# An expert's ten weight splits in gate and up: from groups to even distances

## The chip, the cores and the metric

The kernel runs on one core of one Trainium2 chip. The metric is the device time of one execution in microseconds; lower is better. The median of three runs of the kernel before is 5451.15 us.

## The reference, cut to what matters

A float32 trunk of two layers on 4096 tokens of 1024 channels. Layer 0 mixes with retention and windowed attention, layer 1 with a Fourier transform; behind each mixer stands a mixture of 32 experts, of which each token takes two, and a layer norm. The change touches the experts alone:

```python
def hierarchical_moe(x, w_coarse, b_coarse, w_fine, b_fine, w_gate, w_up, w_down):
    ...
    xs = xt[tok]                       # the tokens, ordered by expert
    hid = jax.nn.silu(lax.ragged_dot(xs, w_gate, sizes)) * lax.ragged_dot(xs, w_up, sizes)
    ys = lax.ragged_dot(hid, w_down, sizes) * gate.reshape(-1)[order][:, None]
    out = jax.ops.segment_sum(ys, tok, num_segments=T)
...
        x = layer_norm(DEEPNORM_ALPHA * x + ffn, ln2_gain[layer], ln2_bias[layer])
```

## The kernel before

Products are made in float32 by three matmuls on split operands: a value `a` is held as a rounded part `h` and a rest `l = a - h`, and `w*x` is taken as `wh*xh + wh*xl + wl*xh`. `Trunk.split` (L77 to L79) makes such a pair with one Copy on ACT (L78) and one subtraction on DVE (L79).

The class `Experts` (L1437) runs the 32 experts of a layer one after the other, each on a fixed number of token slots (168 to 432). An expert has 12 chunks of weights of 512 KB: w0 to w7 for gate and up, w8 to w11 for down. SP's queue loads them in order into four buffers `raw` (`load`, L1486). `split` (L1492) splits the next chunk into its pair in `w[g % 12]` and, as this frees a `raw`, issues the load of the chunk four places on.

Gate and up (`gate_up`, L1540) are four passes over j; pass j uses w(2j) and w(2j+1) and has eight steps k of six matmuls. So there are 32 steps h = 8j + k. At the end of a pass ACT takes Silu (`hid`, L1556), DVE multiplies by the up part (L1557), and `hid` is split into `hth` and `htl`. Down (`down`, L1564) multiplies these by w8 to w11. Between its products stand the transposes of the next expert's tokens (`trans`, L1518): PE transposes into one of two buffers `pt` (L133), ACT and DVE split that into `xth` and `xtl`.

Before the first expert eight chunks are split. Expert e's own part therefore has twelve splits as follows: its own w8 to w11, then w0 to w5 of the next expert, all ten in gate and up, and w6 and w7 in down. The table `at` in `expert` (L1613) says behind which step each of the ten stands.

The order on each engine is that of the code (`manual_schedule`, `run` L1725): an engine does not pass over an instruction that waits. A split that waits for its chunk on ACT therefore holds up the Silu and the `hth` behind it.

In layer 1 the finishing of tokens (`Done`, `plan` L1244) is put into the experts' steps as well. Experts 1 to 7 carry counts and ranks. From expert 9 on an expert carries one tile of 128 finished tokens, some carry two: statistics on DVE behind step 8 (second tile 12), the scaling on ACT behind 16 (20), the gain on POOL behind 18 (22), the bias on DVE behind 22 (26), the store on POOL behind 24 (28).

Of the kernel before, what the change touches and what calls it, by code (L numbers as in the profile page):

```python
# [1436 lines left out]
class Experts:  # L1437
# [63 lines left out]
    def rows(s, e, t):  # L1501
        return max(0, min(P, s.slots[e] - t * P))
# [110 lines left out]
    def expert(s, e):  # L1613

        ix, size = s.idx[e % 5], s.slots[e]
        rows = lambda t: s.rows(e, t)
        late = [f for t in s.tiles(e) if t > 1 for f in s.trans(t, rows(t))] if e else []
        pend, s.pend = s.pend, None
        if e + 3 < E:
            s.index(e + 3)  # L1620
        if pend:
            at = {}
            for i, f in enumerate(late):
                at.setdefault(i if len(late) > 2 else 2 * i + 1, []).append(f)
            pend(at)
        more = e + 1 < E
        steps = []
        if more:
            ix2 = s.idx[(e + 1) % 5]
            for t in s.tiles(e + 1):  # L1630
                s.gather(ix2, t, s.rows(e + 1, t))
            steps = [f for t in range(2) for f in s.trans(t, s.rows(e + 1, t))]
        at = [{2 * i: [s.split] for i in range(4)}]
        at += [{1: [s.split], 3: [s.split]} for _ in range(3)]
        side = {h: list(f) for h, f in s.done.at.get(e, {}).items()} if s.done else {}
        if e == 2:
            side.setdefault(13, []).append(s.excess)
        if s.last(e):
            for t in s.tiles(e):
                side.setdefault(20, []).append(lambda t=t: s.done.fetch(ix, t, t, rows(t)))  # L1640
        for h in [h for h in side if h < 32]:
            at[h // 8].setdefault(h % 8, []).extend(side.pop(h))
        for j in range(4):
            s.gate_up(j, size, at[j])
        steps = [s.split] + steps[:3] + [s.split] + steps[3:]
        at = {2 * i: [f] for i, f in enumerate(steps[:4])}
        for h in [h for h in side if h < 40]:
            at.setdefault(h - 32, []).extend(side.pop(h))
        yo = s.yo[0]
        if s.last(e):  # L1650
            m = rows(2)
            yo0 = s.done.x[4]
            s.down(yo0, ix, 0, at=at)
            s.done.adds(yo0, 0, P, 0)
            if m:
                s.down(s.yo[1], ix, 2, m)
            side = [f for h in sorted(side) for f in side[h]]
            for f in side:
                f()
            first0, second0 = s.done.final_steps(yo0, 0, P)  # L1660
            first0()
            if m:
                s.done.adds(s.yo[1], 2, m, 2)
                first2, second2 = s.done.final_steps(s.yo[1], 2, m)
                first2()
            s.down(yo, ix, 1, rows(1), last=True)
            second0()
            s.done.final(yo, 1, rows(1))
            if m:
                second2()  # L1670
            return
        order = [0, *(t for t in s.tiles(e) if t > 1)]
        for i, t in enumerate(order):
            y = s.yo[(len(order) - i) % 2]
            s.down(y, ix, t, rows(t), at=at if t == 0 else {})
            s.scatter(y, ix, t, rows(t))
        s.down(yo, ix, 1, rows(1), (0,), at={i: [f] for i, f in enumerate(steps[4:])})
        for h in sorted(side):
            for f in side[h]:
                f()  # L1680

        def pending(at={}):
            s.down(yo, ix, 1, rows(1), (1,), at)
            s.scatter(yo, ix, 1, rows(1))
        s.pend = pending
# [214 lines left out]
```

## Time and profile before

| | us |
|---|---|
| median of the runs | 5451.15 (5449.52 to 5457.16) |
| the profiled execution | 5478.56 |
| its span | 5476.9 |
| experts of layer 0 | about 2109 to 3392 of the span |
| experts of layer 1 | about 4072 to 5461 of the span |
| PE busy, ACT, DVE, POOL | 93%, 43%, 62%, 30% |

The profiled execution is 27.4 us above the median, and 1.7 us of it lie outside the span. PE is TensorE; PEclk is its granted clock as a share of the full one. A wait of an engine is its idle time before an instruction; the profile names the instruction that ended it. A duration in a timeline is that of one instruction, and consecutive ones on ACT and DVE start a little closer than their durations.

### The profile page before, as it was taken

What the parts mean: (1) busy time and instruction counts of PE and PEld (TensorE: products, weight loads), DVE (VectorE), ACT (ScalarE), POOL (GpSimd) and SP (SyncE); (2) the same over time, 40 slices, a digit from 0 to 9 for tenths busy, and PEclk for the clock granted to TensorE, in tenths of its full rate; (3) what the DMA queues carried; (4) which work ended last, traced back from release to release, by engine and by line L of the source; (5) the groups of instructions that cost most, each with busy time, mean ns of one, the idle gap of its engine ahead of it and who ended that gap; (6) DMA issues with size and microseconds to landing.
All of it is one profiled execution on the core that took longest, in us unless ns stands there. A gap on an engine that the chain in (4) does not pass through costs nothing. (4 is left out here: it accounts for less than half of the span.)

```text
span 5476.9 us, 85272 instructions
## 1 busy us (share of the span) xinstructions
PE 5087.8 (93%) x32364; PEld 4605.3 (84%) x32364; DVE 3411.8 (62%) x7398; ACT 2380.9 (43%) x4310; POOL 1668.6 (30%) x1556
## 2 busy tenths in 40 slices
PE   9999999799999996999999998889859999999997
PEld 7888888599999986898889887669858888899886
DVE  6777777566666665555544453658865566655665
ACT  4555555322222224555445453552235455555553
POOL 1111111023333332112111211754652243333445
PEclk9999999899999998999999999999969999999998
DMA  4212121433333325776756676775547887777774
GB/s 157 62 61 62 61 63 50 144 105 104 112 102 105 112 90 188 230 231 205 229 154 196 193 234 176 229 254 185 206 159 189 226 236 244 235 218 218 230 227 151
DMA packets 312312, 907.96 MB, mean 166 GB/s; under 512 B 48596, under 2 KB 76420, under 8 KB 311796
## 3 DMA queue, kind: packets, MB, share of 16 engines
q1 hardware_dynamic: 249780, 709.44, 39.3%
q0 software_dynamic: 62096, 192.82, 14.6%
q8 instruction: 259, 4.24, 0.3%
q14 instruction: 177, 1.45, 0.1%
HBM read 678.13 MB, written 226.39 MB: 165 GB/s over the span
## 5 line engine op out<-in xcount | busy, mean ns | idle before, releaser
L1606 POOL DMA_INDIRECT acc_d<-yo,idx x154 | 270.8, 1759 | 1439.7 <-ACT yo L1587 1009.7
L83 PE MATMUL pj<-w1h,xh 128*128 128x512 f32 (+1 forms) x1024 | 396.4, 387 | 8.1 <-ACT w1h L78 6.9
L84 PE MATMUL pj<-w1l,xh 128*128 128x512 f32 (+1 forms) x1024 | 377.9, 369 | 2.3 <-DVE w1l L79 2.2
L85 PE MATMUL pj<-w1h,xl 128*128 128x512 f32 (+1 forms) x1024 | 376.7, 368 | 0.0
L133 PE MATMUL pt<-ident,xg 128*128 128x128 f32 x1256 | 199.2, 284 | 113.8 <-DVE xtl L79 62.1
L133 PEld LDWEIGHTS pt<-ident,xg 128*128 128x128 f32 x1256 | 160.5, 146 | 166.0 <-DVE xtl L79 64.5
L79 DVE TENSOR_TENSOR xtl<-pt,xth 128x512 fp32r<-128x512 f32 (+12 forms) x314 | 184.6, 598 | 162.2 <-ACT xth L78 161.2
L83 PE MATMUL pj<-w2h,xh 128*128 128x384 f32 (+1 forms) x768 | 265.2, 345 | 7.3 <-DVE rb L212 7.1
L1587 ACT ACTIVATE yo<-py,idx 128x512 f32<-128x512 f32 (+6 forms) x256 | 175.8, 687 | 208.2 <-PE py L85 193.1
L83 PE MATMUL po<-woh,cath 128*128 128x354 f32 (+1 forms) x768 | 261.8, 341 | 2.4 <-ACT cath L78 2.0
L85 PE MATMUL po<-woh,catl 128*128 128x354 f32 (+1 forms) x768 | 254.6, 332 | 5.4 <-DVE catl L79 4.2
L84 PE MATMUL pj<-w2l,xh 128*128 128x384 f32 (+1 forms) x768 | 251.8, 328 | 4.0 <-DVE w2l L79 4.0
L78 ACT ACTIVATE hth<-hid 128x256 fp32r<-128x256 f32 (+11 forms) x256 | 104.6, 409 | 345.2 <-DVE hid L1557 344.6
L84 PE MATMUL po<-wol,cath 128*128 128x354 f32 (+1 forms) x768 | 252.9, 329 | 0.0
L85 PE MATMUL pj<-w2h,xl 128*128 128x384 f32 (+1 forms) x768 | 251.3, 327 | 0.0
L78 ACT ACTIVATE ph<-tr 128x384 fp32r<-128x384 f32 (+1 forms) x256 | 122.4, 479 | 285.7 <-PE tr L133 283.3
L1556 ACT ACTIVATE hid<-pgu 128x272 f32<-128x272 f32 (+22 forms) x256 | 97.4, 381 | 339.5 <-PE pgu L1552 335.6
L79 DVE TENSOR_TENSOR pl<-tr,ph 128x384 fp32r<-128x384 f32 (+1 forms) x256 | 139.0, 544 | 133.8 <-ACT ph L78 130.1
L85 PEld LDWEIGHTS pj<-w1h,xl 128*128 128x128 f32 x1024 | 193.8, 189 | 32.7
L1557 DVE TENSOR_TENSOR hid<-hid,pgu 128x272 f32<-128x272 f32 (+22 forms) x256 | 107.8, 421 | 175.1 <-ACT hid L1556 174.9
L83 PEld LDWEIGHTS pj<-w1h,xh 128*128 128x128 f32 x1024 | 194.3, 190 | 23.6 <-ACT w1h L78 8.0
L84 PEld LDWEIGHTS pj<-w1l,xh 128*128 128x128 f32 x1024 | 194.3, 190 | 20.5 <-DVE w1l L79 6.3
(507 smaller groups left out, 18661.9 us busy)
## 6 DMA issues: line engine op xcount, KB each, us to landing
raw<-in_wgu SPq DMA_DIRECT2D x512, 512.0 KB
raw<-in_expert_w_down SPq DMA_DIRECT2D x256, 512.0 KB
xraw<-in_xT SPq DMA_DIRECT2D x64, 512.0 KB
acc_d<-xacc SPq DMA_DIRECT2D x64, 512.0 KB
x<-x_d SPq DMA_DIRECT2D x32, 530.0 KB
xres<-in_x SPq DMA_DIRECT2D x32, 512.0 KB
x_d<-tres SPq DMA_DIRECT2D x32, 512.0 KB
fx<-acc_d SPq DMA_DIRECT2D x32, 512.0 KB
```

Of the source, the lines that this page charges most:

```text
L78: self.nc.scalar.activation(hi, src, AF.Copy)
L79: self.nc.vector.tensor_sub(lo, src, hi)
L83: mm(out, xh, wh, start=start, stop=False)
L84: mm(out, xh, wl, start=False, stop=False)
L85: mm(out, xl, wh, start=False, stop=stop)
L133: self.nc.tensor.transpose(pt[:, k * P:(k + 1) * P], src[:, k * P:(k + 1) * P], self.ident)
L1556: nc.scalar.activation(hid, ps[:, 0, 0:n], AF.Silu)
L1557: nc.vector.tensor_mul(hid, hid, ps[:, 1, 0:n])
L1587: s.nc.scalar.activation(yo[0:m, w], py[i][0:m, :], AF.Copy, scale=gate)
L1606: s.nc.gpsimd.indirect_dma_start(out=s.acc, out_offset=bass.IndirectOffsetOnAxis(ap=ix[0:m, t, 0:1], axis=0), in_=yo[0:m, :], in_offset=No ...
```

## The change

The ten splits in gate and up stand behind other steps; nothing else is changed, and no instruction is added or removed on any engine.

```diff
-        at = [{2 * i: [s.split] for i in range(4)}]
-        at += [{1: [s.split], 3: [s.split]} for _ in range(3)]
+
+        at = [{} for _ in range(4)]
+        for h in (0, 4, 8, 11, 15, 18, 22, 25, 28, 31):
+            at[h // 8].setdefault(h % 8, []).append(s.split)
```

As steps h = 8j + k:

| pass | splits before | chunks | splits after | chunks |
|---|---|---|---|---|
| 0 | 0, 2, 4, 6 | w8, w9, w10, w11 | 0, 4 | w8, w9 |
| 1 | 9, 11 | w0, w1 | 8, 11, 15 | w10, w11, w0 |
| 2 | 17, 19 | w2, w3 | 18, 22 | w1, w2 |
| 3 | 25, 27 | w4, w5 | 25, 28, 31 | w3, w4, w5 |
| down | two | w6, w7 | two | w6, w7 |

Chunks w8 to w11 are the expert's own, w0 to w7 the next one's.

On ACT, in expert 30 of layer 0, the row from w10h to the Silu of pass 2 stood so before (`wNh<-raw` is the ACT half of a split, `hid<-pgu` the Silu of a pass, `hth<-hid` its rounded part):

```order
L78 ACTIVATE w10h<-raw_22133 128x1024
L78 ACTIVATE w11h<-raw_22134 128x1024
L1556 ACTIVATE hid_22171<-pgu_22182 128x208
L78 ACTIVATE hth<-hid_22171 128x208
L78 ACTIVATE w0h<-raw_22131 128x1024
L78 ACTIVATE w1h<-raw_22132 128x1024
L1556 ACTIVATE hid_22172<-pgu_22183 128x208
L78 ACTIVATE hth<-hid_22172 128x208
L78 ACTIVATE w2h<-raw_22133 128x1024
L78 ACTIVATE w3h<-raw_22134 128x1024
L1556 ACTIVATE hid_22171<-pgu_22182 128x208
```

Two splits have moved behind the Silu of pass 0, and w1h and w3h each behind the next Silu. On ACT at the same place now, from the Silu of pass 0:

```order
L1556 ACTIVATE hid_22171<-pgu_22182 128x208
L78 ACTIVATE hth<-hid_22171 128x208
L78 ACTIVATE w10h<-raw_22133 128x1024
L78 ACTIVATE w11h<-raw_22134 128x1024
L78 ACTIVATE w0h<-raw_22131 128x1024
L1556 ACTIVATE hid_22172<-pgu_22183 128x208
L78 ACTIVATE hth<-hid_22172 128x208
L78 ACTIVATE w1h<-raw_22132 128x1024
L78 ACTIVATE w2h<-raw_22133 128x1024
L1556 ACTIVATE hid_22171<-pgu_22182 128x208
```

The Silu of pass 1 no longer has w1h ahead of it, and the Silu of pass 2 no longer has w3h; w3h, w4h and w5h follow, ahead of the Silu of pass 3. On DVE, in expert 12 of layer 1, pass 1 stood so before (`hid<-hid,pgu` is the product of a pass, `dst` the statistics of a finished tile):

```order
L1557 TENSOR_TENSOR hid_50497<-hid_50497,pgu_50508 128x248
L79 TENSOR_TENSOR htl<-hid_50497,hth 128x248
L1329 BN_STATS dst_50534<-dx_50529 128x6 x2
L1330 BN_AGGR dst_50534<-dst_50534 128x2
L101 TENSOR_SCALAR dst_50534<-dst_50534 128x1
L79 TENSOR_TENSOR w0l<-raw_50458,w0h 128x1024
L79 TENSOR_TENSOR w1l<-raw_50459,w1h 128x1024
L1557 TENSOR_TENSOR hid_50498<-hid_50498,pgu_50509 128x248
```

There are two subtractions of weights between the two products of hid. On DVE at the same place now:

```order
L1557 TENSOR_TENSOR hid_50497<-hid_50497,pgu_50508 128x248
L79 TENSOR_TENSOR htl<-hid_50497,hth 128x248
L79 TENSOR_TENSOR w10l<-raw_50460,w10h 128x1024
L1329 BN_STATS dst_50534<-dx_50529 128x6 x2
L1330 BN_AGGR dst_50534<-dst_50534 128x2
L101 TENSOR_SCALAR dst_50534<-dst_50534 128x1
L79 TENSOR_TENSOR w11l<-raw_50461,w11h 128x1024
L79 TENSOR_TENSOR w0l<-raw_50458,w0h 128x1024
L1557 TENSOR_TENSOR hid_50498<-hid_50498,pgu_50509 128x248
```

Three subtractions stand there now, one of them ahead of the statistics.

## Rows read from the trace of the kernel before

**Rows 1.** The page: busy us, share of the span and instructions of each engine.

```profile
PE 5087.8 (93%) x32364; PEld 4605.3 (84%) x32364; DVE 3411.8 (62%) x7398; ACT 2380.9 (43%) x4310; POOL 1668.6 (30%) x1556
```

**Rows 2.** PE's waits, 2109 to 3420: total us, times, longest.

```profile
PE pt L133 <- DVE xtl L79: 16.0, 12, 2.2
```

**Rows 3.** PE's waits, 4072 to 4394.

```profile
PE pt L133 <- DVE xtl L79: 10.3, 6, 2.0
PE pgu L1550 <- DVE hid L1557: 5.9, 2, 3.2
PE py L83 <- ACT hth L78: 3.4, 3, 1.4
```

**Rows 4.** PE's waits, 4394 to 5460.

```profile
PE pt L133 <- DVE xtl L79: 24.6, 13, 4.4
PE py L83 <- ACT hth L78: 11.1, 12, 3.4
```

**Rows 5.** ACT's groups, 2109 to 3400: count, busy, mean ns, idle before, releasers.

```profile
L78 ACT ACTIVATE w1h<-raw 128x1024 fp32r<-128x1024 f32 x31 | 32.8, 1057 | 64.7 <-DMA raw<-in_wgu 64.7
L78 ACT ACTIVATE w3h<-raw 128x1024 fp32r<-128x1024 f32 x31 | 32.7, 1056 | 40.2 <-DMA raw<-in_wgu 40.2
```

**Rows 6.** ACT's groups, 4072 to 4394.

```profile
L78 ACT ACTIVATE w0h<-raw 128x1024 fp32r<-128x1024 f32 x8 | 8.4, 1055 | 18.2 <-DMA raw<-in_wgu 18.2
L78 ACT ACTIVATE w5h<-raw 128x1024 fp32r<-128x1024 f32 x8 | 8.4, 1054 | 7.8 <-DMA raw<-in_wgu 7.8
```

**Rows 7.** ACT's timeline, layer 0, expert 30: start, us, operation, idle before.

```profile
3335.41 1.06 ACT L78 ACTIVATE w1h<-raw 128x1024 fp32r<-128x1024 f32 x1 [4.25 <-DMA raw<-in_wgu]
...
3339.15 1.06 ACT L78 ACTIVATE w2h<-raw 128x1024 fp32r<-128x1024 f32 x1 [0.73 <-DMA raw<-in_wgu]
3342.57 1.06 ACT L78 ACTIVATE w3h<-raw 128x1024 fp32r<-128x1024 f32 x1 [2.36 <-DMA raw<-in_wgu]
...
3347.39 0.33 ACT L1556 ACTIVATE hid<-pgu 128x208 f32<-128x208 f32 x1
3349.24 0.38 ACT L78 ACTIVATE hth<-hid 128x208 fp32r<-128x208 f32 x1 [1.53 <-DVE hid L1557]
```

**Rows 8.** PE's timeline: a wait in layer 0, and down's start and wait in expert 30.

```profile
2696.70 1.01 PE L133 MATMUL pt<-ident,xg 128*128 128x128 f32 x4 [1.84 <-DVE xtl L79]
...
3344.44 0.41 PE L83 MATMUL py<-w8h,hth 128*128 128x512 f32 x1
...
3352.48 0.66 PE L133 MATMUL pt<-ident,xg 128*128 128x128 f32 x4 [1.85 <-DVE xtl L79]
```

**Rows 9.** Stretches behind waits: us, busy of PE, PEld, DVE, ACT, POOL, PEclk, DMA, GB/s.

```profile
2173.94:2177.34 3.40, 3.40 (x12) 2.34 (x13) 1.14 (x2) 2.06 (x3) 0.57 (x1) 0.60 0.50 160
2658.19:2661.59 3.40, 3.40 (x13) 2.47 (x14) 1.38 (x3) 2.12 (x3) 0.98 (x1) 0.67 0.59 171
2696.70:2700.10 3.40, 3.40 (x11) 2.60 (x12) 1.24 (x2) 1.67 (x3) 0.10 (x1) 0.52 0.53 169
...
3352.48:3355.88 3.40, 3.40 (x19) 2.62 (x20) 1.40 (x3) 2.27 (x4) 1.04 (x1) 1.00 0.41 159
```

**Rows 10.** The same columns, expert 0 of layer 1.

```profile
4072.00:4114.00 42.00, 42.00 (x197) 41.69 (x197) 16.52 (x34) 13.67 (x24) 4.22 (x4) 0.51 0.48 158
```

**Rows 11.** The same columns, layer 0, expert 30, where w1h waits.

```profile
3332.00:3336.00 4.00, 4.00 (x38) 4.00 (x38) 0.42 (x1) 0.59 (x1) 0.00 (x0) 1.00 1.02 338
```

**Rows 12.** DVE's timeline, layer 1, expert 12.

```profile
4563.11 1.22 DVE L79 TENSOR_TENSOR w1l<-raw,w1h 128x1024 fp32r<-128x1024 f32 x1
4564.33 0.41 DVE L1557 TENSOR_TENSOR hid<-hid,pgu 128x248 f32<-128x248 f32 x1
...
4567.40 2.49 DVE L79 TENSOR_TENSOR w2l<-raw,w2h 128x1024 fp32r<-128x1024 f32 x1 [1.76 <-ACT w2h L78]
...
4576.66 0.41 DVE L1557 TENSOR_TENSOR hid<-hid,pgu 128x248 f32<-128x248 f32 x1
```

**Rows 13.** POOL's timeline, the same expert.

```profile
4566.41 2.40 POOL L1338 TENSOR_TENSOR dx<-dx,ln2g 128x1024 f32<-128x1024 f32 x1 [1.95 <-ACT dx L1335]
```

## The prediction

> **What bounds the kernel now.** I read the page first: PE is busy 93% of the span, DVE 62% and ACT 43% [rows 1]. So PE's work sets the end, no work is added to it, and the change can be worth only what it does to PE's idle time in the experts, and to the clock behind it. I therefore read PE's waits over three stretches. In layer 0 nearly all of the wait is for one thing: a transpose of the next expert's tokens that waits for its buffer, 12 times and 16.0 us in all, up to 2.2 us [rows 2]. The first eight experts of layer 1 have 10.3 us of that, 5.9 us of gate and up waiting for a product of hid, and 3.4 us of down waiting for hth [rows 3]. The rest of layer 1 has 24.6 and 11.1 us [rows 4]. That is 71 us of a 5478.56 us execution which the change can touch at all.
>
> Why these waits occur is read from ACT's groups: in layer 0 it stands idle 64.7 us ahead of w1h and 40.2 us ahead of w3h, all of it for the load of the chunk [rows 5]; at the start of layer 1 18.2 us ahead of w0h and 7.8 ahead of w5h [rows 6]. As engines keep the order of the code, the Silu behind such a split waits too. Expert 30 of layer 0 shows the whole chain: w1h waits 4.25 us, w2h 0.73, w3h 2.36, each split pushes the next, the last Silu starts at 3347.39 and hth at 3349.24 [rows 7], while PE went on to down at 3344.44; the transpose behind the products waits 1.85 us [rows 8]. hth of pass 3 ends there 5.2 us after PE has left gate and up (3349.24 + 0.38 - 3344.44). I take a wait to shrink or grow one for one with that lag from 5.2 us and 1.85 us, which makes it nothing below 3.3; that is an assumption from this one place.
>
> A wait can cost twice. The stretch of 3.4 us behind a wait of 1.84 us that ends at 2696.70 [rows 8] ran at a granted clock of 0.52, about the lower of the two levels (1.2 and 2.4 GHz), with 11 matmuls; the one behind the 1.85 us of expert 30 ran at 1.00 with 19 [rows 9]. Two more stretches behind long waits of layer 0 had 0.60 and 0.67 [rows 9]. Together these three cost 3.40 x (0.40 + 0.33 + 0.48) = 4.1 us, 1.4 each, which I also take in layer 1.
>
> **The change part by part.** The counts of instructions are the same on every engine, and PE's and POOL's orders too. SP's queue issues the same loads in the same order; each is now issued when a split that stands later is done. What moves are the splits against Silu, product and hth of each pass, and in layer 1 against the steps that finish tokens.
>
> *Loads.* The splits of w10 and w11 move behind the Silu of pass 0, some 4 us, and the loads of w2 and w3, which need their buffers, start that much later. I cost this at nothing: while ACT waits for w1h the DMA engines are already full (share 1.02, 338 GB/s) [rows 11], and w1, w2, w3 come 3.4 to 3.7 us apart [rows 7], so a later issue stands in a queue that is not empty. If that cover were gone, w3 would come up to 4 us later, and the waits would stay as they are.
>
> *Layer 0.* w1h now stands behind the Silu of pass 1 and w3h behind that of pass 2, so the waits for both no longer hold these up. The last Silu still has w3, w4, w5 ahead of it. In expert 30 w3h can start at 3342.6 as before. Before, w4h and w5h started at 3345.49 and 3346.44 without a wait, so w5 lands somewhere between 3342.6 and 3346.4. If it lands late, the Silu stays at 3347.4 and nothing is gained; if early, it starts some 1.9 us sooner and the wait is gone. I take the middle, 0.9 us, since the loads come in an even row. Of the 12 waits [rows 2] six are 1.7 us or longer and make 11.3 us; the six others, 4.7 us, are at most 0.93 each and go wholly. So 4.7 + 6 x 0.9 = 10.1 us. The three stretches at the lower clock go with them, 4.1. Layer 0: **-14.2** (bounds 0 and -(16.0 + 4.1) = -20.1).
>
> *Layer 1, experts 1 to 8.* Pass 0 has two splits ahead of its product where it had four, with w8 and w9 there and no wait for w0h in it: the 5.9 us for hid go. Of the six waits of transposes (10.3 us) and three for hth (3.4) [rows 3] I give 0.9 for four that w0h starts and 1.0 for one hth; those that w5h sets [rows 6] stay, since w5 is split as late as it was. 5.9 + 3.6 + 1.0 = 10.5, and three stretches at the lower clock, 4.2: **-14.7** (bounds 0 and -(19.6 + 4.2) = -23.8).
>
> *Layer 1, experts 9 to 30.* Here DVE is the engine of the chain. In expert 12 pass 1 has the statistics of a tile, then w0l and w1l, then the product at 4564.33 [rows 12]. After the change three subtractions stand ahead of that product, one more of 1.22 us, and ACT's third split starts a little later: I take +1.4 us. In pass 2 the w2l that lasted 2.49 us stood beside POOL's gain, 4566.41 for 2.40 us [rows 13]. In pass 3 there are again three subtractions for two. Carried through, the last product comes at 4579.0 for 4576.66 [rows 12]: +2.3 us, a lag of hth of 5.1 where it was 2.7, so a wait of 5.1 - 3.3 = 1.8 us where there was none. Seven experts have a second tile and wait already: they get the one more subtraction, 7 x 1.2 = 8.4. Experts 10, 11, 13, 14 and 15 have a lag of about 5 us before and after: -0.4 each by the same working, -2.0. Two of the others with few slots get 1.0 each. Longer waits give two more stretches at the lower clock, +2.8. 1.8 + 8.4 - 2.0 + 2.0 + 2.8: **+13.0**. Bounds: 13 experts with a tile have at most 272 slots; 0 below, and if each paid what expert 12 pays, 2.3, and half a stretch at the lower clock, 0.7, +39 above. I stay near the middle of the low half, as experts with more slots have passes long enough for three subtractions.
>
> The page "SBUF — State Buffer" of the Trainium skill, section "Who interferes with whom", says that a DVE instruction with two inputs in SBUF and a GpSimd one that reads SBUF lock each other out; the trace agrees (2.49 us beside POOL's gain, 1.22 for w1l). By that rule each subtraction that newly falls beside a gain would cost 1.27 us more, at most 22 x 1.27 = 28 us for one tile in each of 22 experts, none of which my sum holds.
>
> Sum: -14.2 - 14.7 + 13.0 = -15.9 us. The profiled execution would take 5462.7 for 5478.6, and the runs, from their median 27.4 us below it, 5451.2 - 15.9 = **5435 us**.
>
> **The rivals.**
> *No change.* The loads decide: w3 and w5 come when the queue brings them, so the long waits of layer 0 and of experts 5 to 8 stay, only the short ones (4.7) and those for hid (5.9) go, and experts 9 to 30 give the 13.0 back: -4.7 - 5.9 + 13.0 = +2. For it speak the full DMA engines [rows 11]; against it that the largest idle time, ahead of w1h, is for a chunk now needed 4 us later [rows 5]. It gives 5453, within 10. The Trainium skill, page "DMA: Bandwidth & Descriptors", section "Queues, rings and completion order", says that each DMA engine serves the queues with work in turn; by that rule spreading the splits brings no chunk sooner while gathers share the engines, which the share of 1.02 agrees with and which would leave this rival's 5453.
>
> *More than forecast.* All waits of layer 0 and of experts 1 to 8 go with their stretches, 20.1 + 23.8, and a part of the later 35.7 [rows 4], some 15, as Silu and product come evenly: -59, 5392. Against it speaks pass 3, which now holds three splits ahead of the last hth where it held two.
>
> *Slower.* DVE in layer 1: passes 1 and 3 have three subtractions beside the finishing steps, and the experts of up to 272 slots all pay as expert 12 does, +39, while late loads halve the gain of the two other parts to 14.5: +24.5, 5476. It decides where the loss of experts 9 to 30 exceeds what layer 0 and experts 1 to 8 gain. For it speaks DVE's order; against it, that most of these experts are late already and a wait is paid for the lag beyond 3.3 us only.
>
> One thing stands outside: expert 0 of layer 1 ran 42 us at a clock of 0.51 [rows 10]. Nothing that PE does ahead of it changes, so it stays; a rise a few us sooner or later would move the time by half of that.
>
> **How the numbers follow.** About 0.2%, 10.9 us, is what a measurement of this kernel can tell from no change. Chances: forecast (11 to 35 us less) 0.42, more than that 0.09, no change 0.28, slower 0.21. So faster 0.51, same 0.28, slower 0.21. The range leaves out about half of the slower case and half of the far gain: 5397 to 5471. Of the forecast alone it would be 5416 to 5440.
>
> **What would show it.** In layer 0 ACT's idle time ahead of w1h falls from 64.7 to under 25 us, and PE's waits for xtl from 16.0 to 5 to 7. In experts 1 to 8 the wait for hid is gone. In 4394 to 5460 the two waits together rise from 35.7 to 43 to 47, expert 12 has a wait of about 1.8. I am wrong on the loads if w3h's or w5h's idle time in layer 0 grows by as much as w1h's falls, and wrong on DVE if the waits after 4394 fall.

## The result

The changed kernel took 5477.28 us (median of six runs, 5476.24 to 5490.59) against 5450.34 us of the kernel before on the same chip: a ratio of 1.0057, 95% interval 1.0039 to 1.0074. Run again beside the experiments it was 5497.02 against 5475.32, 1.0050 (1.0033 to 1.0066). The change makes the kernel slower by about 0.5%, 27 and 22 us by the medians. The forecast was 16 us faster, with a range that ended at 5471: wrong in sign, and 6 us outside. The rival "Slower", 5476, came out.

The two profiled executions hide this: 5476.81 us after, 5478.56 before. The extra time of the one before lies ahead of the experts, in code that the change does not touch: its first expert starts at 2109 us, that of after at 2091. So stages have to be compared, not spans. These are the same four stages of the kernel after (layer 0's experts 0 to 30, what lies between the layers, experts 0 to 7 of layer 1, experts 8 to 30), with the duration, the busy time of PE, PEld, DVE, ACT and POOL, PEclk, DMA share and GB/s:

```profile
2091.00:3345.00 1254.00, 1231.19 (x8275) 1117.53 (x8275) 646.94 (x837) 643.92 (x980) 233.42 (x176) 0.99 0.72 209
3345.00:4052.00 707.00, 565.04 (x3433) 505.48 (x3432) 477.55 (x1130) 268.37 (x438) 404.82 (x387) 0.88 0.61 202
4052.00:4372.00 320.00, 301.03 (x2039) 272.96 (x2038) 174.86 (x318) 158.59 (x251) 91.71 (x70) 0.91 0.78 203
4372.00:5402.00 1030.00, 977.05 (x6278) 872.10 (x6277) 620.35 (x805) 530.42 (x807) 401.13 (x332) 0.97 0.75 225
```

and of the kernel before:

```profile
2109.00:3360.00 1251.00, 1232.85 (x8277) 1119.00 (x8276) 646.50 (x837) 646.59 (x981) 244.70 (x176) 0.99 0.71 210
3360.00:4071.00 711.00, 567.17 (x3433) 507.21 (x3432) 477.10 (x1131) 267.77 (x438) 405.72 (x387) 0.88 0.60 201
4071.00:4394.00 323.00, 300.80 (x2034) 273.50 (x2033) 174.22 (x318) 157.94 (x249) 82.94 (x70) 0.91 0.76 200
4394.00:5403.00 1009.00, 969.87 (x6277) 870.69 (x6277) 618.47 (x805) 531.34 (x807) 394.43 (x331) 0.98 0.76 230
```

The engines do the same work. The last stage alone is clearly longer, by 21 us, and layer 0 has gained nothing. PE's waits in the kernel after, from 2109 to 3420, then 4072 to 4394, then 4394 to 5460 (total us, times, longest), which answer to [rows 2 to 4]:

```profile
PE pt L133 <- DVE xtl L79: 20.1, 16, 2.2
```

```profile
PE pt L133 <- DVE xtl L79: 11.4, 7, 1.9
PE py L83 <- ACT hth L78: 4.7, 4, 1.8
PE pgu L1550 <- DVE hid L1557: 1.9, 2, 1.7
```

```profile
PE pt L133 <- DVE xtl L79: 26.9, 16, 2.0
PE py L83 <- ACT hth L78: 23.6, 16, 2.6
```

Layer 0 went from 16.0 to 20.1 us where 5 to 7 was expected. From 4394 on, the two waits together went from 35.7 to 50.5, where 43 to 47 was expected. ACT's groups in layer 0 after (count, busy us, mean ns, idle before and its releaser), for [rows 5]:

```profile
L78 ACT ACTIVATE w3h<-raw 128x1024 fp32r<-128x1024 f32 x31 | 32.4, 1044 | 0.0
...
L78 ACT ACTIVATE w2h<-raw 128x1024 fp32r<-128x1024 f32 x30 | 31.7, 1056 | 78.6 <-DMA raw<-in_wgu 78.6
L78 ACT ACTIVATE w1h<-raw 128x1024 fp32r<-128x1024 f32 x30 | 31.4, 1048 | 6.9 <-DMA raw<-in_wgu 6.8
```

Of the 64.7 us ahead of w1h 6.9 are left, and the 40.2 ahead of w3h are gone, as forecast; but 78.6 us now stand ahead of w2h, where there had been 7.

The stages of all profiled executions follow, in us, taken from PE's timeline from the first gate and up matmul of one expert to that of another. Each kernel has one such execution, but kernels with the same code in a layer repeat each other, and the scatter can be read from them. "e" are experts; the splits are named by pass. In the column of layer 1, "even" is 2, 3, 2, 3 as in the change and "groups" 4, 2, 2, 2 as before.

| execution | layer 0 | layer 1 | layer 0, e0-30 | layer 1, e0 | e1-7 | e8-30 |
|---|---|---|---|---|---|---|
| before | groups | groups | 1250.7 | 52.9 | 270.1 | 1009.4 |
| l0_even | even | groups | 1249.5 | 53.8 | 268.0 | 1005.7 |
| group_r8 | groups, 8 buffers | groups | 1228.9 | 33.8 | 270.0 | 1000.6 |
| after | even | even | 1253.9 | 53.8 | 265.5 | 1030.5 |
| even_again | even | even | 1250.8 | 33.7 | 273.6 | 1027.5 |
| l1_even | groups | even | 1247.7 | 53.7 | 268.0 | 1029.6 |
| even_r8 | even, 8 buffers | even | 1225.7 | 53.0 | 268.0 | 1023.6 |
| even_stats0 | even | even, statistics in pass 0 | 1247.0 | 54.0 | 271.4 | 1005.2 |
| s2332 | 2, 3, 3, 2 | 2, 3, 3, 2 | 1260.0 | 53.7 | 275.2 | 1028.5 |
| s3223 | 3, 2, 2, 3 | 3, 2, 2, 3 | 1238.3 | 54.3 | 268.2 | 1002.2 |
| s4123 | 4, 1, 2, 3 | 4, 1, 2, 3 | 1237.7 | 53.8 | 268.2 | 997.7 |
| best_a | even, 8 buffers | 4, 1, 2, 3 | 1227.5 | 54.3 | 264.7 | 997.6 |
| best_b | 4, 1, 2, 3, 8 buffers | 4, 1, 2, 3, statistics in pass 0 | 1227.3 | 34.2 | 280.2 | 1002.9 |
| best_c | even, 8 buffers | 3, 2, 2, 3, statistics in pass 0 | 1227.0 | 53.9 | 268.6 | 1001.4 |

For e8-30 the three with groups have a mean of 1005.2 (1000.6 to 1009.4) and the four with the change's code 1027.8 (1023.6 to 1030.5): the change costs 22.6 us there. In layer 0 and in e1-7 it moves nothing beyond the scatter.

### The profile page after: what moved, and what is told of

It is laid out like the page before. It is cut to its first block, busy times and chain, and to the rows that moved or that the text cites. A ratio compares the mean times of both kernels' runs of the same rounds, so it can differ in the third digit from the quotient of the medians.

```text
span 5475.1 us, 85270 instructions
## 1 busy us (share of the span) xinstructions
PE 5089.2 (93%) x32364; PEld 4606.0 (84%) x32364; DVE 3411.8 (62%) x7398; ACT 2379.1 (43%) x4310; POOL 1672.5 (31%) x1556
```

## The experiments

Two theories stood against each other. A: DVE and ACT hold three splits ahead of one Silu or product, and in layer 1 finishing steps beside them. B: since w10 and w11 are split later, the loads that need their buffers start later. All ratios are to the kernel before, run beside the kernel on the same chip.

### Which layer

```diff
-        for h in (0, 4, 8, 11, 15, 18, 22, 25, 28, 31):
+        for h in ((0, 2, 4, 6, 9, 11, 17, 19, 25, 27) if s.layer else (0, 4, 8, 11, 15, 18, 22, 25, 28, 31)):
```

> Even distances in layer 0 only, groups as before in layer 1. The traces of before and after put the experts of layer 0 at 1250.7 and 1253.9 us, so either theory wants about +3 us on 5450, within 10: 5453. If the loss sat in late loads of w2 (layer 0 shows 78.6 us of waits for it), it would show here as +10 or more.

Measured: 5472.87 against 5472.92, ratio 1.0001 (0.9984 to 1.0017). Its mirror image has the two lists exchanged:

> Even distances in layer 1 only. Theory A (DVE and ACT hold three splits ahead of one Silu, beside the finishing steps): nearly the whole loss is here, +18 to +24 us, about 5471. Theory B (the loads of w2 and w3 are issued late because w10 and w11 are split late): the loss is shared between the layers, under +15 here.

Measured: 5497.10, ratio 1.0038 (1.0022 to 1.0054), so 21 us by the ratio and 24 by the medians. The loss is in layer 1.

### Which pass

```diff
-        for h in (0, 4, 8, 11, 15, 18, 22, 25, 28, 31):
+        for h in (0, 4, 8, 11, 15, 17, 19, 22, 25, 27):
```

> Splits of the ten by pass 2, 3, 3, 2 (w8 w9, then w10 w11 w0, then w1 w2 w3, then w4 w5): as the change, but w3 goes ahead of the Silu of pass 2, so pass 3 has two splits as before the change. Theory A, with pass 3 as the place: 15 to 25 us less than the change, 5452 to 5462. Theory A with pass 1 as the place, or theory B: as the change, 5477 within 6.

Measured: 5516.91, ratio 1.0086 (1.0062 to 1.0110). That is neither of the two: taking one split out of pass 3 made the kernel slower still. w3 now stands ahead of the Silu of pass 2 and waits there. ACT's groups in layer 0 of this kernel:

```profile
L78 ACT ACTIVATE w3h<-raw 128x1024 fp32r<-128x1024 f32 x31 | 32.8, 1059 | 12.1 <-DMA raw<-in_wgu 12.0
L78 ACT ACTIVATE w2h<-raw 128x1024 fp32r<-128x1024 f32 x31 | 32.8, 1057 | 82.6 <-DMA raw<-in_wgu 82.6
```

The 82.6 us ahead of w2h are those of the change, and layer 0 takes 1260.0 us. In e8-30 this kernel takes 1028.5 us, as the change does, though pass 3 has only two splits again. Since pass 2 has three here, that alone does not clear pass 3; the next run does. It goes in the other direction, with w10 back in pass 0:

```diff
-        for h in (0, 4, 8, 11, 15, 18, 22, 25, 28, 31):
+        for h in (0, 3, 6, 9, 11, 18, 22, 25, 28, 31):
```

> By pass 3, 2, 2, 3 (w8 w9 w10, w11 w0, w1 w2, w3 w4 w5): w10 is split in pass 0 as before, pass 1 has two splits, pass 3 keeps the three of the change. Theory A with pass 3 as the place: as the change, 5477 within 6. Theory A with pass 1 as the place: 5450 to 5460. Theory B: the load of w2 is issued as early as before, its 78.6 us of waits in layer 0 fall below 45, and the time to about 5462.

Measured: 5457.67, ratio 0.9974 (0.9957 to 0.9991): not only no loss, but faster than the kernel before, and 1002.2 us in e8-30 with three splits still in pass 3. So pass 3 with three splits is not the place of the loss. In layer 0:

```profile
L78 ACT ACTIVATE w2h<-raw 128x1024 fp32r<-128x1024 f32 x31 | 32.7, 1053 | 29.2 <-DMA raw<-in_wgu 29.1
```

w2's wait fell to 29.2 us, as theory B wants; but pass 1 also has one split less, as theory A with pass 1 wants. The runs that follow separate these, one layer at a time.

### Loads alone, in layer 0

```diff
+        s.NRAW = 4 if layer else 8
```

With eight raw buffers a load waits for the split eight places ahead and not four. Layer 1 keeps its four.

> The change as it is, with eight raw buffers for four in layer 0, so that a load no longer waits for the split of the chunk four places ahead. Theory B (in layer 0 the late splits of w10 and w11 make the load of w2 late): the waits for raw in layer 0, 87.6 us after the change, fall below 15, and its experts take 10 us or more less than the 1253.9 of the change; the whole about 0.2 to 0.3% over the kernel before. Rival (the shared DMA engines set when a chunk lands): waits and time as with the change, 0.4 to 0.6% over.

Measured: 5444.85 against 5448.09, ratio 0.9995 (0.9978 to 1.0011). That is no longer slower than the kernel before, where 0.2 to 0.3% over it was expected. ACT's groups and PE's wait (2109 to 3375) in layer 0:

```profile
L78 ACT ACTIVATE w2h<-raw 128x1024 fp32r<-128x1024 f32 x31 | 32.4, 1044 | 0.0
```

```profile
PE pt L133 <- DVE xtl L79: 2.2, 1, 2.2
```

> The kernel before with eight raw buffers in layer 0. Theory B: the 125.7 us of waits for raw in layer 0 fall below 20, PE's waits there from 16 to about 4, and the time is 0.2 to 0.35% below the kernel before. Rival (DMA engines): no change within 0.1%.

Measured: 5423.52, ratio 0.9957 (0.9939 to 0.9974). The same holds: no wait for a chunk, 2.2 us of PE's wait. So in layer 0 all but one of PE's waits for xtl came from chunks that were late (the one left, 2.2 us, stands ahead of expert 10 in every execution), and the chunks were late because their buffer was: issued early enough, the same DMA engines bring every chunk in time. With the buffers there, each of the experts 1 to 30 takes the same time under both orders within 0.1 us (expert 30: 34.3 and 34.3). With the loads early, three splits in pass 1 and in pass 3 cost nothing in layer 0. The 0.38% by which even_r8 stays behind group_r8 is again the loss of layer 1.

### The statistics alone, in layer 1

```diff
-        def tile(k, i, b, eg, hg, ec, hc, at=(0, 8, 10, 14, 16)):
+        def tile(k, i, b, eg, hg, ec, hc, at=(-6, 8, 10, 14, 16)):
```

> The change, with the statistics of a finished tile moved six steps ahead on DVE, into pass 0, which has two splits now; scale, gain, bias and store stay. Theory A (in layer 1 pass 1 has three splits beside the statistics, and that makes the product late): experts 8 to 30 of layer 1 fall from 1030.5 by 8 us or more, the whole to 0.2 to 0.35% over the kernel before. If three splits in pass 1 cost as much without the statistics: as the change, 0.4 to 0.6% over.

Measured: 5463.08 against 5448.09, ratio 1.0022 (1.0005 to 1.0039), and 1005.2 us in e8-30 where the change has 1027.8 and the groups 1005.2. That is one execution, but it is 18 us below the lowest of the four with the change's code. The splits, loads and buffers are those of the change; only the statistics left pass 1. DVE's timeline of expert 12 in the kernel after (start, us, operation):

```profile
4539.12 0.41 DVE L1557 TENSOR_TENSOR hid<-hid,pgu 128x248 f32<-128x248 f32 x1 [1.91 <-ACT hid L1556]
...
4540.97 1.23 DVE L79 TENSOR_TENSOR w10l<-raw,w10h 128x1024 fp32r<-128x1024 f32 x1 [0.54 <-ACT w10h L78]
4542.11 1.28 DVE L1329 BATCH_NORM_STATS2 dst<-dx 128x6 f32<-128x512 f32 x2
...
4543.75 1.23 DVE L79 TENSOR_TENSOR w11l<-raw,w11h 128x1024 fp32r<-128x1024 f32 x1
4544.89 1.22 DVE L79 TENSOR_TENSOR w0l<-raw,w0h 128x1024 fp32r<-128x1024 f32 x1
4546.03 0.40 DVE L1557 TENSOR_TENSOR hid<-hid,pgu 128x248 f32<-128x248 f32 x1
```

and in even_stats0:

```profile
4545.49 0.41 DVE L1557 TENSOR_TENSOR hid<-hid,pgu 128x248 f32<-128x248 f32 x1 [0.24 <-ACT hid L1556]
...
4547.34 1.23 DVE L79 TENSOR_TENSOR w10l<-raw,w10h 128x1024 fp32r<-128x1024 f32 x1 [0.54 <-ACT w10h L78]
4548.48 1.22 DVE L79 TENSOR_TENSOR w11l<-raw,w11h 128x1024 fp32r<-128x1024 f32 x1
4549.61 1.22 DVE L79 TENSOR_TENSOR w0l<-raw,w0h 128x1024 fp32r<-128x1024 f32 x1
4550.99 0.41 DVE L1557 TENSOR_TENSOR hid<-hid,pgu 128x248 f32<-128x248 f32 x1 [0.16 <-ACT hid L1556]
```

From one product to the next DVE takes 6.9 us in the first and 5.5 in the second, where it even waits 0.16 us for the Silu; PE's passes start 5.5 us apart in this expert. Behind that product stand hth, then on ACT the scaling of the tile and the split of w1, so the 1.4 us pass on. The products of the four passes come 6.14, 13.04, 21.67 and 26.91 us after the expert's start in the kernel after, and 6.14, 11.64, 19.39 and 24.63 in even_stats0: 1.4 us arise in pass 1, and 0.9 more in pass 2, where w2h waits 2.3 us for its load after and 1.4 in even_stats0. ACT's timeline of the kernel after shows pass 1: the Silu starts at 4544.22, and hth waits 1.87 us for the product.

```profile
4544.22 0.38 ACT L1556 ACTIVATE hid<-pgu 128x248 f32<-128x248 f32 x1 [1.39 <-PE pgu L1552]
4546.46 0.41 ACT L78 ACTIVATE hth<-hid 128x248 fp32r<-128x248 f32 x1 [1.87 <-DVE hid L1557]
4546.78 1.23 ACT L1335 ACTIVATE dx<-dx,dst 128x1024 f32<-128x1024 f32 x1
```

Could late loads, theory B, cost layer 1 its 22.6 us as well? ACT's waits for chunks in e8-30 speak against it. They went down with the change, from 47.0 us before (4394 to 5403) to 19.6 after (4372 to 5402), in these groups above all:

```profile
L78 ACT ACTIVATE w1h<-raw 128x1024 fp32r<-128x1024 f32 x23 | 24.3, 1056 | 28.5 <-DMA raw<-in_wgu 28.5
```

```profile
L78 ACT ACTIVATE w2h<-raw 128x1024 fp32r<-128x1024 f32 x23 | 24.2, 1051 | 13.4 <-DMA raw<-in_wgu 13.3
```

In even_stats0 w2h even waits 21.2 us there, and the stage is short all the same. So theory A with pass 1 holds for the loss of layer 1, which needs both the third split and the statistics in one pass (s3223 takes away the split, even_stats0 the statistics), and theory B for what holds layer 0 back. The time does not come back to that of the kernel before, though: 0.22% is left, by the interval at least 0.05%. The stages of this execution do not show where; that is open.

### Fewer splits in pass 1, and the versions put together

```diff
-        for h in (0, 4, 8, 11, 15, 18, 22, 25, 28, 31):
+        for h in (0, 2, 4, 6, 11, 18, 22, 25, 28, 31):
```

> Ten splits by pass 4, 1, 2, 3 (w8 to w11 in pass 0 as before the change, w0 in pass 1, w1 and w2, then w3 to w5). If the moved splits of w10 and w11 are what costs, and the later w1 and w3 what gains, this is better than 3, 2, 2, 3: 0.3 to 0.5% below the kernel before, waits for raw in layer 0 below 50 us. Rival: four splits in pass 0 bring the wait for the product of hid back in experts 2 and 4 of layer 1 (5.9 us) and it is only 0.1 to 0.25% below.

Measured: 5432.30 against 5448.09, ratio 0.9968 (0.9950 to 0.9986). Layer 0 has 27.5 us of waits ahead of w2h and 52.5 for all chunks, just over the 50 that was expected; the rival's wait for the product of hid, 5.9 us before, is 2.2. The kernel is as good as 3, 2, 2, 3 within the intervals, with the four splits in pass 0 of the kernel before. So four splits in pass 0 were not what held the kernel before back. Against it w1 has left pass 1 and w3 pass 2, and w0, w2, w4 and w5 stand a few steps later; which of these shifts helps was not tried apart.

> The change itself once more, beside the others of this row on one chip: 0.4 to 0.7% over the kernel before.

Measured: 1.0050, as told above. On the same chip, the versions put together:

> Even distances with eight raw buffers in layer 0, and 4, 1, 2, 3 splits by pass in layer 1. If the parts add up (layer 0: 1225.7 for 1250.7; experts 8 to 30 of layer 1: 997.7 for 1009.4) about 36 us, 0.6 to 0.7% below the kernel before. If the gain of a faster layer 0 is lost elsewhere, as 4, 1, 2, 3 alone, 0.3%.

Measured: 5440.63 against 5475.32, ratio 0.9939 (0.9920 to 0.9958). The parts add up: 1227.5 us in layer 0, 997.6 in e8-30.

> 4, 1, 2, 3 in both layers, eight raw buffers in layer 0, and the statistics in pass 0. Pass 0 has four splits and the statistics then: if a DVE pass so full costs what the full pass 1 did, experts 8 to 30 of layer 1 are 10 us or more above the 997.7 that they take without the moved statistics; if only what stands behind it counts, they are equal or better.

Measured: 5437.32, ratio 0.9935 (0.9914 to 0.9956), with 1002.9 us in e8-30: 5 us more than without the moved statistics, less than the 10 that a full pass was to cost, and not the equal or better of the other reading; single executions of one code differ by 7 to 9 us in this stage, so it decides nothing.

> Even distances with eight raw buffers in layer 0, and in layer 1 3, 2, 2, 3 by pass with the statistics in pass 0 (three splits there). Moving the statistics took 25 us from the change (1030.5 to 1005.2 in experts 8 to 30); with two splits in pass 1 there is less to take: 5 to 10 us below the 1002.2 of 3, 2, 2, 3, the whole 0.6 to 0.8% below the kernel before. If the statistics cost nothing once pass 1 has two splits: 0.5%.

Measured: 5443.45, ratio 0.9945 (0.9926 to 0.9964), with 1001.4 us in e8-30 for the 1002.2 of 3, 2, 2, 3. Once pass 1 has two splits, moving the statistics is worth nothing that shows. best_a, b and c are equal by their intervals, and all three beat both kernels.

## Why the prediction was wrong

**Loads: the step that failed.** The prediction cost the later loads of w2 and w3 at nothing, because the DMA engines were full at 3332 to 3336 [rows 11], and took from this that a later issue would stand in a queue that is not empty. That row was read from the one stretch where a load was already late. Ahead of it the engines had not been full all along. While SP waited for the split of w8 (done at 3326.12), and until the load issued behind it moved bytes, they stood nearly idle in the kernel before (the columns of [rows 9]):

```profile
3324.90:3327.60 2.70, 2.70 (x27) 2.70 (x26) 2.70 (x3) 2.70 (x3) 2.39 (x1) 1.00 0.19 49
```

In expert 30 of the kernel before, w10l, which frees the buffer of w2, began at 3327.17 and ended 5.4 us after the expert's start (3323.02); after, it starts at 3316.61 and ends 9.0 us after the start (3308.86):

```profile
3316.61 1.23 DVE L79 TENSOR_TENSOR w10l<-raw,w10h 128x1024 fp32r<-128x1024 f32 x1 [0.57 <-ACT w10h L78]
```

SP's waits in that expert show who holds the load up: 4.3 us for w10l after,

```profile
SPq L1490 <- DVE w10l L79: 4.3, 1, 4.3
```

and 0.7 before,

```profile
SPq L1490 <- DVE w10l L79: 0.7, 1, 0.7
```

Over the 4.3 us the DMA share was 0.98, at 194 GB/s, and 0.58 in their last 2.3. So the load of w2 is issued 3.6 us later. Chunk w2 could be split 16.1 us after the expert's start before [rows 7] and 17.8 after, where it now sits ahead of the Silu of pass 2: of the 3.6 us the queue covered some 1.9, and 1.7 were not covered. ACT's timeline after, against [rows 7]:

```profile
3326.65 1.06 ACT L78 ACTIVATE w2h<-raw 128x1024 fp32r<-128x1024 f32 x1 [2.98 <-DMA raw<-in_wgu]
3327.62 0.33 ACT L1556 ACTIVATE hid<-pgu 128x208 f32<-128x208 f32 x1
...
3329.57 1.04 ACT L78 ACTIVATE w3h<-raw 128x1024 fp32r<-128x1024 f32 x1
3330.63 1.06 ACT L78 ACTIVATE w4h<-raw 128x1024 fp32r<-128x1024 f32 x1
3331.90 1.06 ACT L78 ACTIVATE w5h<-raw 128x1024 fp32r<-128x1024 f32 x1 [0.20 <-DMA raw<-in_wgu]
3332.86 0.33 ACT L1556 ACTIVATE hid<-pgu 128x208 f32<-128x208 f32 x1
3334.53 0.38 ACT L78 ACTIVATE hth<-hid 128x208 fp32r<-128x208 f32 x1 [1.34 <-DVE hid L1557]
```

The wait that was to vanish with w1 stands before w2 instead, and the three splits behind it leave ACT no slack to catch up: 5.2 us between the two Silus, as long as a pass (PE's four take 21.4). The prediction had named this case, "If that cover were gone, w3 would come up to 4 us later, and the waits would stay as they are": the cover was half gone, the chunk was w2 and not w3, and the waits stayed, 16.0 us before and 20.1 after. PE's timeline after shows down's start and the wait of expert 30, against [rows 8]:

```profile
3330.28 0.41 PE L83 MATMUL py<-w8h,hth 128*128 128x512 f32 x1
...
3337.77 0.65 PE L133 MATMUL pt<-ident,xg 128*128 128x128 f32 x4 [1.59 <-DVE xtl L79]
```

It went from 1.85 to 1.59 us, not to 1.0. The lag of hth was 4.6 (3334.53 + 0.38 - 3330.28): by the line of lag less 3.3 that would be 1.3. One for one was right, but the line was drawn through a place where the wait no longer grows. Taken over layer 0's experts, this wait is about the lag less 3.05 (expert 13 after: 3.91 and 0.88; expert 14 after: 4.62 and 1.58) and stays at 1.85 from a lag of 4.9 on (before: 5.15 and 1.85 in expert 14, 5.47 and 1.84 in expert 15; after: 6.19 and 1.85 in expert 1). A lag of over 4.9 has to fall below that before any of the wait goes.

**Layer 0, -14.2: measured about 0.** (1250.7 and 1247.7 under groups, 1253.9, 1249.5, 1250.8 and 1247.0 under even distances.) With the loads early, layer 0 takes 19 to 28 us less than these (1228.9 for groups, 1225.7 for even distances), about the bound of 20.1 that was given or more.

**Layer 1, experts 1 to 8, -14.7: measured about 0 in e1-7.** The step on hid held in the main: 5.9 us became 1.9. But the waits for transposes went from 10.3 to 11.4 and for hth from 3.4 to 4.7, where 3.6 and 1.0 were to go. The prediction gave the wait for hid to the product of pass 0. It stands ahead of w6h, where pass 3 starts and needs the buffer that the product of pass 1 frees; here in expert 2 of the kernel before:

```profile
4180.00 0.36 PE L1550 MATMUL pgu<-xth,w6h 128*128 128x200 f32 x1 [3.23 <-DVE hid L1557]
```

w1 has left the place ahead of that product, w0 has not. ACT still waits 15.6 us for w0h in these eight experts, where it waited 18.2, and for all chunks 34.0, where it was 35.5: the loads come no sooner, so the waits that hang on them stay. Which of PE's waits hang on w0h was not tried apart.

**Layer 1, experts 9 to 30, +13.0: measured +22.6 in e8-30.** The mechanism and the place were right (one more subtraction beside the statistics in pass 1), the size too small. In expert 12 the product of pass 1 came 1.4 us later, as forecast, and the last one 2.9 later (26.91 us after the expert's start for 23.97), where 2.3 was forecast; it got 2.4 us of waits for 1.8, and the seven experts with two tiles 11.0 more for 8.4. In the traces of before and after the stage differs by 21.1 us: PE's waits went from 38.5 to 52.5, and PE's busy time rose by 7.2 for the same matmuls at a granted clock of 0.97 for 0.98, where 2.8 us were allowed. Pass 3 was held to be the worse place; s3223 shows that three splits there cost nothing that can be seen, since it takes 1002.2 us in this stage.

**The lock of DVE and POOL** was not worth anything. From the rule on the page "SBUF — State Buffer" of the Trainium skill, section "Who interferes with whom", the prediction had estimated at most 28 us; the slow subtractions only changed their names. DVE's groups after, 4409 to 5347:

```profile
L79 DVE TENSOR_TENSOR w1l<-raw,w1h 128x1024 fp32r<-128x1024 f32 x21 | 54.3, 2587 | 34.9 <-ACT w1h L78 34.9
L79 DVE TENSOR_TENSOR w2l<-raw,w2h 128x1024 fp32r<-128x1024 f32 x21 | 40.9, 1948 | 1.7 <-ACT w2h L78 1.7
```

and before, 4429 to 5350:

```profile
L79 DVE TENSOR_TENSOR w2l<-raw,w2h 128x1024 fp32r<-128x1024 f32 x21 | 54.3, 2585 | 34.9 <-ACT w2h L78 34.9
L79 DVE TENSOR_TENSOR w3l<-raw,w3h 128x1024 fp32r<-128x1024 f32 x21 | 40.9, 1947 | 0.4 <-ACT w3h L78 0.4
```

Each time it is the subtraction beside the gain of the first tile, or of the second, that meets it. It takes about 2.6 us beside the gain of the first tile, in each of 21 experts, and 3.4 beside that of the second, in the seven that have one, where the other subtractions of a chunk take 1.22. That agrees with the rule.

**The rivals.** "Slower" had the right result for half of the right reason: DVE's passes with finishing steps, which it priced at 39 us where 22.6 was measured, against a gain of the other parts that it halved to 14.5 and that was in truth nothing. That its 5476 met the measured time is in part luck, as the two errors cancel. "No change" had the right view of layer 0, that the waits stay, but not the right reason: it put them on the full DMA engines, and even_r8 and group_r8 show that it is the buffers.

## What to carry to other kernels

Where a transfer's issue waits for a buffer, moving the step that frees the buffer moves the transfer. DMA engines that are full at the moment of the late load do not excuse it: look at the engines and at the issuing queue in the microseconds ahead, where they may stand idle. When work is spread evenly over stages, count per stage what else is queued on each engine there; an even number of one kind of work made the stage with the statistics overfull. Where the even spread lost 0.5%, the same splits with the frees kept early and the late chunks moved back (4, 1, 2, 3 or 3, 2, 2, 3) gave 0.3%, the order of before with more buffers in layer 0 gave 0.4%, and more buffers in layer 0 with one of these orders in layer 1 gave 0.6%.

## What was not expected of the hardware

Expert 0 of layer 1 takes either 33.7 to 34.2 or 52.9 to 54.3 us, and which of the two does not follow the kernel: the change had 53.8 in one execution and 33.7 in another. The prediction had set this expert aside as one that stays as it is [rows 10]. It is PE's granted clock. In the kernel after and in its second execution (duration, busy time of the engines, PEclk, DMA share, GB/s):

```profile
4052.40:4106.20 53.80, 53.80 (x252) 50.91 (x251) 20.92 (x41) 19.17 (x33) 8.23 (x7) 0.59 0.46 146
```

```profile
4075.60:4109.30 33.70, 33.70 (x253) 31.11 (x252) 20.56 (x41) 19.26 (x33) 3.67 (x3) 0.97 0.77 221
```

In the 15.6 us ahead of it PE was busy for 3.5 us in the one and 3.6 in the other and had a clock of 0.50 in both; what decides between them is not shown. These 20 us, a third of a percent, come and go in single executions, about as much as the change itself costs, and are one reason to compare executions stage by stage.
